# The low parts of the expert weights: GpSimd's quarter goes to VectorE

## The chip, the cores and the metric

The kernel runs on one core of one Trainium2 chip. The metric is the device time of one execution in microseconds (us), the median of several runs. The engines are TensorE (PE in the profile, its weight loads PEld), VectorE (DVE), ScalarE (ACT), GpSimd (POOL) and SyncE (SP), which issues DMAs.

## The reference

One layer of a decoder over 1024 tokens of width 1024, all in fp32. Three sublayers follow each other: token mixing (sparse attention beside a recurrent mixer), cross-attention into 256 memory tokens, and a mixture of experts. Only the last one matters here:

```
s = sigmoid(x @ router_w)                      # 16 experts, in 4 groups
group = best group of each token; e = its top-2 experts
gate = s[e] / sum(s[e])
y = sum over the two e of gate * ((silu(x @ w_gate[e]) * (x @ w_up[e])) @ w_down[e])
x = layer_norm(alpha * x + y)
```

Each of the 16 experts has three weights of 1024 x 512 values, 2 MB each.

## The kernel before

**Split products.** A product of fp32 matrices is made of three matrix multiplications on rounded values. A value v is split into a high part, hi = v rounded to the type fp32r, and a low part, lo = v - hi. `mm3` (L35 to L37) sums hi*hi, hi*lo and lo*hi into one PSUM bank; for some rows two products are enough (L1591, L1639, L1640).

**The experts.** `Experts.load` (L1519) fetches half of a weight, 1 MB, from HBM into a buffer `wraw` of 128 x 2048 values, by a DMA on SyncE's queue. `parts` forms its hi (`whi`) and lo (`wlo`) in CUT = 4 pieces of 128 x 512: ScalarE casts a piece to `whi` (L1528), then VectorE or GpSimd subtracts (L1529):

```
for i in range(CUT):
    cs = slice(n * i, n * i + n)
    nc.scalar.copy(hi[:, cs], raw[:, cs])
    (nc.gpsimd if i in LOPOOL else nc.vector).tensor_tensor(lo[:, cs], raw[:, cs], hi[:, cs].bitcast(F32), ALU.subtract)
```

There are 16 experts x 6 halves x 4 pieces = 384 such pieces; 8 of them are formed early, near 1364 us, while the cross-attention's output is still under way (`early`). The others go LOOK = 4 halves ahead of their use. Two halves of a weight, eight pieces, are taken as a pair.

**One expert** (`expert`). Its tokens are gathered by an indirect DMA of GpSimd (`exg`, L1551) once GpSimd has worked out their indices in five small steps (`ef` and `eix`, L1542 to L1546). TensorE turns them (`etp`, L1558), ScalarE and VectorE split them into `exh` and `exl` by `split` (L28; for the second set of rows into the two halves of `exr`), TensorE multiplies with gate and up weights (`eacc`), ScalarE and VectorE form silu times up (`eth`, L1578, L1579, L1601), which is turned and split into `ehh` and `ehl` (`ehr` for the second set), and multiplied with the down weight. ScalarE scales the result (`ey`, L1627) and GpSimd adds it to the sum in HBM by an indirect DMA (`accd`, L1632). Eight experts have a second, smaller set of rows. After the last experts the layer norm runs over the rows of `accd` (statistics `lnst` L978, then L987 and L992), and the last two experts' rows are normed on their own and scattered to the output (L1635).

**Order.** The code is traced in the order in which it is written, and a planner (`schedule_with_timeline_sim=True`) then lays out the instructions of each engine by its own costs and due times. Each engine runs its instructions in the order laid out.

Of the kernel before, what the change touches and what calls it, by code (L numbers as in the profile page):

```python
# [1252 lines left out]
GROUPS = (4, 7, 8)  # L1253
FIRST = (14, 6, 6, 6, 6, 6, 6, 7)
HOLD = 4
CUT, LOPOOL = 4, (2,)
LATE = 2


# [653 lines left out]
```

## Time and profile before

| | us |
|---|---|
| median of 3 runs | 1892.65 |
| lowest, highest | 1884.31, 1894.74 |
| profiled execution | 1896.58 |
| its span, first to last instruction | 1894.7 |
| busy: PE, DVE, ACT, POOL | 1759.3, 1321.1, 858.6, 698.1 |
| mean granted TensorE clock, of full speed | 0.959 |

The profiled execution is one further run. Its span is what the profile's views divide up; its own time is 1.9 us longer. The experts' products run from about 1430 us to 1866 us, and the layer norm at the end overlaps the last ones.

### The profile page before, as it was taken

Reading aid. Unit: us, or ns where it says so; the run is one execution under the profiler, and the core shown is the slowest. Engines: PE = TensorE matmul, PEld = TensorE weight load, DVE = VectorE, ACT = ScalarE, POOL = GpSimd, SP = SyncE. Lnnn points to the kernel's source line nnn. Section 1 sums busy time; section 2 is a strip of 40 time slices with the busy share of each in tenths; the row PEclk is TensorE's granted clock in tenths of the full one; section 3 lists DMA queues with packets and bytes.
Section 4 is the critical chain, followed back from the end, with each engine's and each line's share of the span. In section 5 each row is a group of like instructions: output and inputs, shape, how many; then the busy total and the mean of one; then the engine's idle time right before and its main releaser. Section 6 shows DMA issues by size and latency. Waiting matters only on the chain. (4 is left out here: it accounts for less than half of the span.)

```text
span 1894.7 us, 27396 instructions
## 1 busy us (share of the span) xinstructions
PE 1759.3 (93%) x9158; PEld 1433.4 (76%) x9158; DVE 1321.1 (70%) x2767; ACT 858.6 (45%) x1775; POOL 698.1 (37%) x780
## 2 busy tenths in 40 slices
PE   8999999999999899999999789999998999999991
PEld 6877777777687787888887577878787888877871
DVE  3225876888777621498987575546987788989876
ACT  4223313434332222298887441024414666667662
POOL 1123202221221121175747122100346576656556
PEclk9999989999999899999999899999989999999995
DMA  7363434444432226812101765133325999899984
GB/s 232 110 186 105 118 142 124 135 128 121 108 111 87 67 89 198 255 43 75 46 8 36 226 211 172 34 97 123 117 107 172 332 325 309 278 294 302 332 269 152
DMA packets 246143, 301.98 MB, mean 159 GB/s; under 512 B 54653, under 2 KB 142741, under 8 KB 245488
## 3 DMA queue, kind: packets, MB, share of 16 engines
q1 hardware_dynamic: 238016, 273.59, 44.4%
q0 software_dynamic: 7984, 26.62, 5.7%
q8 instruction: 73, 1.20, 0.3%
q14 instruction: 70, 0.57, 0.1%
HBM read 234.05 MB, written 70.98 MB: 161 GB/s over the span
## 5 line engine op out<-in xcount | busy, mean ns | idle before, releaser
L1529 DVE TENSOR_TENSOR wlo<-wraw,whi 128x512 fp32r<-128x512 f32 x288 | 281.1, 1026 | 26.1 <-ACT whi L1528 25.7
L35 PE MATMUL acc<-xh,wh 128*128 128x512 f32 (+1 forms) x656 | 273.6, 417 | 5.9 <-ACT wh L117 3.0
L36 PE MATMUL acc<-xl,wh 128*128 128x512 f32 (+1 forms) x656 | 267.1, 408 | 0.0
L37 PE MATMUL acc<-xh,wl 128*128 128x512 f32 (+1 forms) x656 | 266.6, 408 | 0.2 <-POOL wl L118 0.2
L1528 ACT CAST whi<-wraw 128x512 fp32r<-128x512 f32 x384 | 207.8, 623 | 35.4 <-PE eacc L1591 10.2
L118 POOL TENSOR_TENSOR wl<-wraw,wh 128x1024 fp32r<-128x1024 f32 (+1 forms) x41 | 100.8, 2459 | 308.6 <-ACT wh L117 259.2
L35 PEld LDWEIGHTS acc<-xh,wh 128*128 128x128 f32 (+1 forms) x656 | 125.1, 191 | 45.3 <-issue 8.0
L1529 POOL TENSOR_TENSOR wlo<-wraw,whi 128x512 fp32r<-128x512 f32 x96 | 138.8, 1482 | 46.4 <-ACT whi L1528 40.5
L37 PEld LDWEIGHTS acc<-xh,wl 128*128 128x128 f32 (+1 forms) x656 | 124.6, 190 | 33.7 <-issue 5.2
L36 PEld LDWEIGHTS acc<-xl,wh 128*128 128x128 f32 (+1 forms) x656 | 125.0, 191 | 29.8 <-issue 3.1
L851 DVE TENSOR_TENSOR tinv<-xinv,ln 128x248 f32<-128x248 f32 (+30 forms) x248 | 89.3, 360 | 40.6 <-DMA ln<-ld 15.6
L475 ACT ACTIVATE pp<-pp,nm 128x640 f32<-128x640 f32 (+7 forms) x128 | 94.3, 740 | 9.3 <-DVE nm L474 8.1
L28 DVE TENSOR_TENSOR pl<-ptp,ph 128x512 fp32r<-128x512 f32 x132 | 87.4, 685 | 12.0 <-ACT ph L28 11.3
L36 PE MATMUL eacc<-wlo,exh 128*128 128x512 f32 x240 | 94.2, 392 | 0.2 <-DVE wlo L1529 0.2
L35 PE MATMUL eacc<-whi,exh 128*128 128x512 f32 x240 | 94.2, 393 | 0.0
L37 PE MATMUL eacc<-whi,exl 128*128 128x512 f32 x240 | 94.2, 392 | 0.0
L480 POOL TENSOR_SCALAR pp<-pp,wgt 128x640 f32<-128x640 f32 (+7 forms) x128 | 88.4, 711 | 0.6
L852 DVE TENSOR_TENSOR xinv<-xinv,tinv 128x248 f32<-128x248 f32 (+30 forms) x248 | 84.0, 339 | 5.9
L980 POOL TENSOR_SCALAR lnrs<-lnmv 128x1 f32<-128x1 f32 x21 | 19.7, 936 | 180.5 <-DVE lnmv L979 172.6
L28 ACT CAST ph<-ptp 128x512 fp32r<-128x512 f32 x132 | 73.8, 583 | 16.9 <-PE ptp L534 16.1
L534 PE MATMUL ptp<-ident,pp 128*128 128x128 f32 x528 | 79.2, 276 | 0.4 <-DVE pl L28 0.2
L909 ACT COPY state<-rseq 64x64 f32<-64x64 f32 x128 | 26.8, 209 | 116.4 <-PE rseq L905 97.5
(502 smaller groups left out, 4542.9 us busy)
## 6 DMA issues: line engine op xcount, KB each, us to landing
wraw<-in_moe_w_up SPq DMA_DIRECT2D x32, 1024.0 KB
wraw<-in_moe_w_gate SPq DMA_DIRECT2D x32, 1024.0 KB
wraw<-in_moe_w_down SPq DMA_DIRECT2D x32, 1024.0 KB
wraw<-in_w_in SPq DMA_DIRECT2D x40, 512.0 KB
sm<-ev SPq DMA_DIRECT2D x32, 256.0 KB
sr<-ev SPq DMA_DIRECT2D x28, 256.0 KB
skew<-skew SPq DMA_DIRECT2D x1, 4608.0 KB
xraw<-in_x SPq DMA_DIRECT2D x8, 512.0 KB
```

The source lines that it names most:

```text
L28: x = nc.scalar.copy(hi, src), (nc.gpsimd if by_pool else nc.vector).tensor_tensor(lo, src, hi.bitcast(F32), ALU.subtract)
L35: nc.tensor.matmul(out, ah, bh, start=start, stop=False)
L36: nc.tensor.matmul(out, ah, bl, start=False, stop=False)
L37: nc.tensor.matmul(out, al, bh, start=False, stop=stop)
L118: nc.gpsimd.tensor_tensor(wl, raw, wh.bitcast(F32), ALU.subtract)
L475: nc.scalar.activation(pt[:, :n], pt[:, :n], AF.Exp, bias=nm, scale=-1.0, accum_out=sums[:, 0, i:i + 1])
L480: nc.gpsimd.tensor_scalar(st[br, i][:, :n], st[br, i][:, :n], w[:, 0, i:i + 1], 1.0, ALU.mult, ALU.mult)
L534: nc.tensor.transpose(tp[:, 128 * i:128 * i + 128], st[br, i][:, c0:c0 + 128], ident)
L851: nc.vector.tensor_tensor(tmp[:, :, :w], x[:, :, j:j + 1].to_broadcast([128, 8, w]), ln[:, j:j + 1, j + 1:].to_broadcast([128, 8, w]), ALU ...
L852: nc.vector.tensor_tensor(x[:, :, j + 1:], x[:, :, j + 1:], tmp[:, :, :w], ALU.subtract)
L1528: nc.scalar.copy(hi[:, cs], raw[:, cs])
L1529: (nc.gpsimd if i in LOPOOL else nc.vector).tensor_tensor(lo[:, cs], raw[:, cs], hi[:, cs].bitcast(F32), ALU.subtract)
```

## The change

The constant that tells which of the four pieces go to GpSimd is emptied. Piece 2 of each half, 96 in all, is now subtracted by VectorE like the other three. Nothing else in the code changes; the planner lays out all instructions anew.

```diff
 HOLD = 4
-CUT, LOPOOL = 4, (2,)
+CUT, LOPOOL = 4, ()
 LATE = 2
```

## Rows read from the trace of the kernel before

**Rows 1.** The page's head: the span, and busy time, share of the span and instructions of each engine.
```profile
span 1894.7 us, 27396 instructions
PE 1759.3 (93%) x9158; PEld 1433.4 (76%) x9158; DVE 1321.1 (70%) x2767; ACT 858.6 (45%) x1775; POOL 698.1 (37%) x780
```

**Rows 2.** Busy time by stretch: the stretch, its length, busy us (and instructions) of PE, PEld, DVE, ACT, POOL, then the granted clock, the DMA engines' busy share and GB/s.
```profile
1445.00:1838.00 393.00, 382.95 (x1824) 313.90 (x1824) 333.09 (x396) 268.74 (x516) 246.33 (x248) 0.99 0.94 303
...
1640.00:1690.00 50.00, 47.49 (x225) 39.31 (x224) 44.51 (x49) 31.14 (x61) 29.77 (x32) 0.97 0.96 298
...
1840.00:1895.00 55.00, 14.00 (x48) 9.99 (x48) 39.04 (x43) 18.27 (x29) 33.37 (x29) 0.65 0.55 186
```

**Rows 3.** What TensorE waits for from 1445 to 1838 us (total us, times, longest), and the row of its timeline at 1441 us (start, us; in brackets the idle time before it and what ended it).
```profile
PE etp L1558 <- DMA exg<-x2d,eix: 3.2, 2, 2.5
PE eacc L1639 <- DVE ehr L28: 2.7, 6, 0.9
PE eacc L1591 <- DVE exr L28: 2.1, 2, 1.7
PE etp L1558 <- PE etp L1558: 1.0, 2, 0.8
PE eacc L35 <- ACT ehh L28: 0.7, 1, 0.7
PE eacc L36 <- DVE wlo L1529: 0.2, 1, 0.2
...
1441.21 1.97 PE L1558 MATMUL etp<-ident,exg 128*128 128x128 f32 x8 [5.01 <-DMA exg<-x2d,eix]
```

**Rows 4.** The low parts: the page's groups by engine (count | busy us, mean ns | idle before), and from the tile's own view the least, median and greatest duration in ns.
```profile
L1529 DVE TENSOR_TENSOR wlo<-wraw,whi 128x512 fp32r<-128x512 f32 x288 | 281.1, 1026 | 26.1 <-ACT whi L1528 25.7
L1529 POOL TENSOR_TENSOR wlo<-wraw,whi 128x512 fp32r<-128x512 f32 x96 | 138.8, 1482 | 46.4 <-ACT whi L1528 40.5
...
L1529 DVE TENSOR_TENSOR wlo<-wraw,whi x288: 639/682/4751, 1363.6 to 1845.1; 128x512 fp32r<-128x512 f32 x144
L1529 POOL TENSOR_TENSOR wlo<-wraw,whi x96: 1261/1357/1861, 1364.7 to 1837.9; 128x512 fp32r<-128x512 f32 x96
```

**Rows 5.** Timeline, merged runs (start, us, count): a run of two low parts on VectorE with none on GpSimd beside it, a run of six, and GpSimd's low parts beside that run.
```profile
1560.14 1.29 DVE L1529 TENSOR_TENSOR wlo<-wraw,whi 128x512 fp32r<-128x512 f32 x2 [2.77 <-ACT whi L1528]
...
1652.31 7.93 DVE L1529 TENSOR_TENSOR wlo<-wraw,whi 128x512 fp32r<-128x512 f32 x6
...
1655.31 3.77 POOL L1529 TENSOR_TENSOR wlo<-wraw,whi 128x512 fp32r<-128x512 f32 x3
```

**Rows 6.** Timeline of VectorE, GpSimd and TensorE near 1364 us, where the first pieces are formed.
```profile
1364.84 3.98 DVE L1529 TENSOR_TENSOR wlo<-wraw,whi 128x512 fp32r<-128x512 f32 x3
1368.74 0.68 DVE L1236 SCALAR_TENSOR_TENSOR x<-x,xwo 128x512 f32<-128x512 f32 x1
...
1366.79 1.48 POOL L1529 TENSOR_TENSOR wlo<-wraw,whi 128x512 fp32r<-128x512 f32 x1 [0.80 <-ACT whi L1528]
...
1369.46 0.50 PE L35 MATMUL xwo<-xoh 128*128 128x512 f32 x1 [1.69 <-DVE x L1236]
```

**Rows 7.** The same near 1461 us.
```profile
1461.60 5.86 DVE L1529 TENSOR_TENSOR wlo<-wraw,whi 128x512 fp32r<-128x512 f32 x6
...
1465.44 1.48 POOL L1529 TENSOR_TENSOR wlo<-wraw,whi 128x512 fp32r<-128x512 f32 x1 [2.01 <-ACT whi L1528]
...
1467.85 0.51 PE L1591 MATMUL eacc<-whi,exr 128*128 128x512 f32 x1 [1.68 <-DVE exr L28]
```

**Rows 8.** Timeline of ScalarE, GpSimd and TensorE, 1638 to 1661 us: the result y, GpSimd's queue up to the next gather, and the turn that needs it.
```profile
1638.00 0.69 ACT L1627 ACTIVATE ey<-eacc,ef 128x512 f32<-128x512 f32 x1
...
1639.91 1.29 POOL L1529 TENSOR_TENSOR wlo<-wraw,whi 128x512 fp32r<-128x512 f32 x1
...
1641.29 1.28 POOL L1529 TENSOR_TENSOR wlo<-wraw,whi 128x512 fp32r<-128x512 f32 x1
1642.74 1.87 POOL L1632 DMA_INDIRECT accd<-ey,eix  x1 [0.17 <-issue]
...
1653.49 0.18 POOL L1543 CAST eix<-ef 128x1 int32<-128x1 f32 x1 [3.67 <-DMA accd<-ey,eix]
...
1654.24 1.05 POOL L1551 DMA_INDIRECT exg<-x2d,eix  x1 [0.44 <-POOL eix L1546]
...
1660.77 2.20 PE L1558 MATMUL etp<-ident,exg 128*128 128x128 f32 x12 [2.51 <-DMA exg<-x2d,eix]
```

**Rows 9.** Timeline of VectorE and GpSimd where the last low parts are formed.
```profile
1839.04 1.29 DVE L978 BATCH_NORM_STATS2 lnst<-wraw 128x6 f32<-128x512 f32 x2 [6.24 <-DMA wraw<-accd]
...
1840.83 1.28 DVE L1529 TENSOR_TENSOR wlo<-wraw,whi 128x512 fp32r<-128x512 f32 x2
...
1836.60 2.54 POOL L1529 TENSOR_TENSOR wlo<-wraw,whi 128x512 fp32r<-128x512 f32 x2
```

**Rows 10.** What SyncE's queue waits for from 1440 to 1845 us (total us, times, longest).
```profile
SPq L1519 <- DVE wlo L1529: 165.6, 71, 8.5
```

**Rows 11.** GpSimd's small steps: one kind of index step from 1445 to 1838 us (count | busy us, mean ns), one of them alone at 1435 us, and the gathers' least, median and greatest duration in ns.
```profile
L1544 POOL TENSOR_SCALAR ef<-ef,dum 128x1 f32<-128x1 f32 x20 | 13.3, 664 | 1.3
...
1435.01 0.34 POOL L1544 TENSOR_SCALAR ef<-ef,dum 128x1 f32<-128x1 f32 x1
...
L1551 POOL DMA_INDIRECT exg<-x2d,eix x23: 1017/1053/1493, 1436.8 to 1806.4; - x23
```

## Prediction

> **What bounds the kernel now.** I read the page's busy shares first [rows 1], then the table of stretches [rows 2] to find the stage that the change touches, then what TensorE waits for in that stage [rows 3], and last the changed instructions themselves [rows 4 to 11]. The page alone says that TensorE is busy for 93% of the span and VectorE for 70%. The stretch 1445 to 1838 us, which is the experts' stage after its start, says more: TensorE is busy 382.95 of 393 us, VectorE 333.09, ScalarE 268.74, GpSimd 246.33, and the DMA engines 94% [rows 2]. So TensorE sets this stage and VectorE has 60 us of room in it. What the change can give there is bounded by TensorE's idle time: 3.2 + 2.7 + 2.1 + 1.0 + 0.7 + 0.2 = 9.9 us, plus what a lowered clock costs behind an idle stretch. Of these waits only 0.2 us are for a low part itself; the others are for small conversions by VectorE (ehr, exr) and for gathered rows (exg) [rows 3].
>
> The reader should see next that the low part has two speeds on VectorE: its median is 682 ns, its mean 1026 and its maximum 4751 [rows 4]. The long ones lie beside GpSimd's low parts: a run of two without GpSimd takes 1.29 us, a run of six takes 7.93 us while GpSimd makes three of its own in 3.77 us [rows 5]. Over 288 the excess is 288 x (1.026 - 0.682) = 99 us of VectorE's time.
>
> The Trainium skill names the mechanism in "SBUF — State Buffer", section "Who interferes with whom": a VectorE instruction with two SBUF inputs contends with a GpSimd instruction that reads SBUF, and the later one blocks until the first is done. This trace agrees, with 682 ns without and up to 4751 ns beside such a neighbour.
>
> **The change part by part.** It takes 96 low parts off GpSimd, which are 138.8 us of its busy time (mean 1482 ns) [rows 4], and adds 96 to VectorE. No byte, matmul, cast or DMA changes in number.
>
> *Price of one on VectorE.* In a run two take 1.29 us [rows 5] and a single one 0.68 [rows 4], so one more costs 0.61. The upper bound is what one occupies on average today, 281.1 / 288 = 0.976 us [rows 4]. I take 0.61, since GpSimd's neighbour, which makes it 0.976, is gone. VectorE then spends 384 x 0.61 = 234 us on low parts instead of 281: it is relieved by 47 us although it makes a third more of them. A set of eight (two halves of a weight) takes 8 x 0.61 = 4.9 us where six take 6 x 0.976 = 5.9 on average. VectorE stays off the bound: 333 - 47 = 286 of 393 us.
>
> The Trainium skill, "VectorE: DVE Perf Modes", section "The TRN2 errata", has a formula for an fp32 two-input instruction that gives 691 ns for 512 elements, and its section on the drain lets no next one start before. By that the 384 would take 265 us, an estimate. The rows show that the next one starts after 0.61 us in a run; by either price VectorE is relieved.
>
> *What this gives, place by place.*
> 1. Start of the parts, at 1364 us: three low parts take 3.98 us beside GpSimd's, the x behind them starts at 1368.74, and TensorE waits 1.69 us for it [rows 6]. With GpSimd's part among them there are four at 0.61, which ends at 1367.3: -1.5 us.
> 2. At 1461 us: six take 5.86 us, and TensorE waits 1.68 us for the exr behind them [rows 7]. Eight take 4.9: -1.0 us.
> 3. The other waits for ehr and exr come to 2.7 + 2.1 - 1.7 = 3.1 us [rows 3]. The runs ahead of them lie beside GpSimd's low parts as well; I take two thirds: -2.0 us.
> 4. The gather at 1654.24 us. Its chain runs back over GpSimd's in-order queue: the rows y were ready at 1638.69, but the scatter started only at 1642.74, with two low parts ahead of it (1639.91 and 1641.29, together 2.57 us). The next index waits until 1653.49 for that scatter's DMA, then comes the gather, and TensorE stands 2.51 us [rows 8]. Without the two low parts the scatter leaves some 2.5 us sooner, and so does all behind it: -2.5 us. The granted clock of that stretch is 0.97 [rows 2]; the missing 3% of 50 us are 1.5 us, which come back with the wait: -1.5 us.
> 5. The other gather that TensorE waits for has 3.2 - 2.5 = 0.7 us [rows 3]: -0.7 us.
> 6. The end. Two of GpSimd's low parts at 1836.60 lie beside VectorE's waiting time; VectorE does its last ones behind the statistics of 1839.04, which wait 6.24 us for a load [rows 9]. From there to the end VectorE is the busiest (39.04 of 55 us) [rows 2], so two more in its queue cost up to 2 x 0.61: +1.2 us. The cover for them would be the idle 6.24 us ahead, if they stand before the statistics; I don't count on it.
>
> Sum: -1.5 - 1.0 - 2.0 - 4.0 - 0.7 + 1.2 = -8.0 us. The 5.01 us wait at 1441 us stays: its gather goes out before GpSimd has made any low part of this stage [rows 3].
>
> *Work costed at nothing.* The loads of raw weights start when a buffer comes free, and SyncE waits 165.6 us for VectorE's low parts [rows 10]; sooner frees make earlier loads. That gives nothing, since no wait of TensorE is for a weight beyond the 0.2 us. If this cover went, the DMA engines at 94% would be next. What is queued behind the added low parts on VectorE is eth, exl, exr, ehl and ehr; TensorE waits for those.
>
> **Rivals.**
> *More comes back.* TensorE loses nearly all its idle time of the stage (9.9 us), the 1.5 us of clock, the 1.5 us of place 1, and the end gains about 3 us as well because the scatters ahead of it leave sooner: about -16 us, 1877. For it: each place has GpSimd in its chain. Against it: waits for transposes and for ScalarE (1.0 + 0.7 us) do not.
>
> *Nothing that can be seen.* The stage is 97% TensorE and the gathers are paced by the scatters' landings, so that an earlier scatter meets another wait: 0 to -3 us, about 1891. For it: only 9.9 us are there to take, in many small places.
>
> *Slower by VectorE's queue.* The order of instructions is written by a planner that reckons with the costs of each engine, so the added low parts can be placed ahead of a conversion that TensorE needs soon, and where no GpSimd part slowed VectorE, eight take 1.2 us longer than six. The place is the experts' loop, 48 sets of eight. If a third of the sets cost TensorE 1.2 us, that is 16 x 1.2 = +19 us against the -8: +11, about 1904. It decides from seven sets on (7 x 1.2 = 8.4). If the low part even kept its 0.976 us, the 94 in the stretch would bring VectorE to 333 + 92 = 425 of 393 us and it would become the bound: +32 us, 1925. That decides from where an added low part costs VectorE over (393 - 333) / 94 = 0.64 us with the others at today's price. Against both: the long ones have GpSimd's beside them, which goes.
>
> *Slower by GpSimd's small steps.* A denser stream on VectorE holds up the index arithmetic and the descriptors on GpSimd. For it: an index step of one column takes 0.34 us alone and 664 ns on average in this stage, and the gather takes from 1017 to 1493 ns [rows 11]. If each of five steps and the gather lost another 0.68 us, a gather would be 4 us late; at the six or so that come just in time this is 6 x 4 = +24 us less the 8: +16, 1909. It decides where the added delay exceeds the 2.5 us that the two low parts free. Against it: VectorE's time in low parts falls, from 281 to 234 us.
>
> The Trainium skill has this rule, in "SBUF — State Buffer", section "SBUF: two separate sides": VectorE's instructions that hold the shared ports keep GpSimd from writing descriptors, so that a DMA issued there looks blocked. It ties that to a mode which this instruction does not have, so I give it a small chance.
>
> **How the numbers follow.** The profiled execution took 1896.58 us, 1.9 more than its span and 3.9 more than the median of the three runs. Its sum is 1896.6 - 8.0 = 1888.6; the same step from the median 1892.65 gives 1884.6, and I say 1885. Chances: this forecast 0.42 (its own range 1878 to 1891), more comes back 0.30, nothing 0.10, VectorE's queue 0.10, GpSimd's steps 0.08. Half a percent, 9.5 us, is about what a measurement can tell here (the three runs spread over 10.4 us). Faster by more than that: 0.30 and a fifth of the forecast, 0.38. Slower: 0.18. Within: 0.44. The range runs from 1868 (9.9 us of idle time, 1.5 of clock, 1.5 of place 1, 5 at the end, and 7 for the scatter of the runs, whose lowest is 8.3 below their median) to 1904 (the mild case of VectorE's queue); what lies outside is part of the slow cases and a little below, under 0.2.
>
> **What would show it.** Right: low parts on VectorE with mean near their median of 682 ns and no maximum above 1 us; VectorE's busy time in 1445 to 1838 down by some 40 us; no wait for exg near 1660 us and the clock there at 1.00. Wrong: a mean still near 1 us; waits for ehl, ehr or exr that grow; gathers that take longer; or a TensorE busy time and end of stage that stand where they were.

## The result, and the profile after

The changed kernel takes 1917.47 us (median of 4 runs, 1914.59 to 1920.21) beside 1893.0 of the kernel before on the same chip: ratio 1.0138, 95% interval 1.0103 to 1.0174. It is slower by 24.5 us where I forecast 8 us less. The profiled execution took 1915.71 us.

The page's head of the changed kernel and its groups of low parts, and from the tile's own view their least, median and greatest duration:

```profile
span 1913.9 us, 27190 instructions
PE 1752.1 (92%) x9158; PEld 1429.2 (75%) x9158; DVE 1279.3 (67%) x2863; ACT 858.4 (45%) x1775; POOL 568.8 (30%) x684
...
L1529 DVE TENSOR_TENSOR wlo<-wraw,whi 128x512 fp32r<-128x512 f32 x384 | 238.0, 683 | 33.3 <-ACT whi L1528 33.3
...
L1529 DVE TENSOR_TENSOR wlo<-wraw,whi x384: 642/683/700, 1350.7 to 1859.8; 128x512 fp32r<-128x512 f32 x192
```

Beside [rows 1, 4] the change does what it says. VectorE makes a third more low parts in 238.0 us instead of 281.1, none is longer than 700 ns, and GpSimd has lost 129 us. No engine got more to do, and the kernel is longer. So the time must be waiting. The same stretches as in [rows 2], and what TensorE waits for as in [rows 3]:

```profile
1445.00:1838.00 393.00, 368.48 (x1738) 304.19 (x1737) 273.89 (x461) 251.03 (x482) 105.58 (x142) 0.97 0.88 287
1640.00:1690.00 50.00, 49.34 (x239) 40.68 (x239) 38.29 (x65) 35.52 (x69) 17.20 (x25) 1.00 0.97 317
```

```profile
PE etp L1558 <- DMA exg<-x2d,eix: 22.3, 6, 6.1
PE eacc L1639 <- DVE ehr L28: 1.8, 4, 1.1
PE eacc L1591 <- DVE exr L28: 0.4, 1, 0.4
```

TensorE was busy for 382.95 of these 393 us and is now busy for 368.48. The waits for VectorE's conversions fell (ehr and exr from 4.8 to 2.2 us), those for gathered rows grew from 3.2 to 22.3, and the granted clock went from 0.99 to 0.97. Where the time is lost is told by three timelines.

**A. The order on TensorE.** The end of one expert and the turns of the next, first in the kernel before, then in the changed one:

```profile
1704.54 1.90 PE L1610 MATMUL etq<-ii,egr 128*128 128x64 f32 x16
1706.24 0.48 PE L35 MATMUL eacc<-whi,ehh 128*128 128x512 f32 x1
...
1712.78 1.06 PE L1558 MATMUL etp<-ident,exg 128*128 128x128 f32 x8 [0.70 <-DMA exg<-x2d,eix]
```

```profile
1704.68 1.90 PE L1610 MATMUL etq<-ii,egr 128*128 128x64 f32 x16
1711.73 1.09 PE L1558 MATMUL etp<-ident,exg 128*128 128x128 f32 x4 [5.16 <-DMA exg<-x2d,eix]
1712.47 0.78 PE L35 MATMUL eacc<-whi,ehh 128*128 128x512 f32 x1
...
1720.25 1.47 PE L1558 MATMUL etp<-ident,exg 128*128 128x128 f32 x12
```

Before, the 24 down products (ehh, ehl) came first, and the gathered rows landed while they ran. Now the planner has put four turns of the next expert's rows ahead of those ready products. TensorE works through its queue in order, so it stands 5.16 us for a gather that lands no later than before (1711.60 against 1712.64). The products behind it then run at the lower of the clock's two levels at first: 0.78 us for the first one, where it was 0.48. The changed kernel has this order at four places, and at three of them (1604, 1711, 1820 us) TensorE waits 5.2 to 6.1 us.

**B. The start.** GpSimd, VectorE and TensorE of the changed kernel where the first expert's tokens are gathered, then busy times by stretch (columns as in [rows 2]) where that gather lands, of after and of before:

```profile
1421.73 5.13 POOL L1544 TENSOR_SCALAR ef<-ef,dum 128x1 f32<-128x1 f32 x1
1426.81 0.18 POOL L1546 CAST eix<-ef 128x1 int32<-128x1 f32 x1
1427.14 1.04 POOL L1551 DMA_INDIRECT exg<-x2d,eix  x1 [0.15 <-POOL eix L1546]
...
1421.92 4.89 DVE L1529 TENSOR_TENSOR wlo<-wraw,whi 128x512 fp32r<-128x512 f32 x8
...
1434.75 1.97 PE L1558 MATMUL etp<-ident,exg 128*128 128x128 f32 x8 [14.31 <-DMA exg<-x2d,eix]
```

```profile
1430.00:1445.00 15.00, 9.21 (x38) 7.65 (x39) 6.35 (x12) 5.97 (x12) 5.67 (x15) 0.65 1.02 381
```

```profile
1436.00:1445.00 9.00, 3.92 (x13) 3.03 (x13) 4.32 (x15) 2.75 (x6) 5.11 (x15) 0.70 0.33 75
```

An index step of one column, 0.34 us when alone [rows 11], lasts 5.13 us: it ends (1426.86) with VectorE's unbroken run of eight low parts beside it (1426.81). The gather leaves 4.8 us late, at 1427.14. By then the loads of the next weights go out as well (1427.40 and 1430.13), the DMA engines are full (1.02 from 1430 on, against 0.33), and the gather needs 7.6 us to land where before it needed 4.4 (issued at 1436.80, landed by 1441.21). That the loads slow it is my reading; the gather of [rows 8], in the full stage of the kernel before, needed 6.4 us too. The wait of 5.01 us [rows 3] has become 14.31.

**C. The end.** VectorE and GpSimd of the changed kernel, then of the kernel before; TensorE's last instruction ends at 1880.2 and 1866.0 us:

```profile
1886.64 3.36 DVE L992 SCALAR_TENSOR_TENSOR wraw<-wraw,lnrs,eexr 128x1024 f32<-128x1024 f32 x1 [2.22 <-POOL lnrs L981]
1889.93 0.74 DVE L1629 SCALAR_TENSOR_TENSOR exg<-eacc,ef,exg 128x512 f32<-128x512 f32 x1
...
1896.94 1.75 POOL L1635 DMA_INDIRECT out<-exg,eix  x1 [0.53 <-issue]
```

```profile
1870.55 3.36 DVE L987 SCALAR_TENSOR_TENSOR exg<-exg,lnmv,exgr 128x1024 f32<-128x1024 f32 x1
1873.84 1.40 DVE L1629 SCALAR_TENSOR_TENSOR exg<-eacc,ef,exg 128x512 f32<-128x512 f32 x2
...
1877.30 1.04 POOL L1635 DMA_INDIRECT out<-exg,eix  x1 [0.83 <-DVE exg L992]
```

The first of the two last scatters goes out 16.7 us after TensorE's end instead of 11.3: the last result is added (L1629) later, behind another row block's norm (L992), and more of the norm stands behind it. The tail from TensorE's last instruction to the end of the trace is 33.7 us instead of 28.7.

The profile's sum: between the first product of a gathered second set (exr) and TensorE's last instruction lie 441.7 us instead of 422.7 (+19.0), the tail has +5.0. The first such product comes 4.8 us earlier (1438.5 against 1443.3), in spite of B, since the work ahead of the experts ran some 13 us earlier in this execution: its first output product of the cross-attention (`xwo`) starts at 1301.6 us instead of 1314.3, when no low part has been formed yet. A kernel with the old split shows such an early start too (1434.5 in e6), so I give that to neither side. 19.0 + 5.0 - 4.8 = 19.2, the difference of the spans.

### The profile page after: what moved, and what is told of

Same layout as the page of the kernel before. It is cut to its first block, busy times and chain, and to the rows that moved or that the text cites. A ratio compares the mean times of both kernels' runs of the same rounds, so it can differ in the third digit from the quotient of the medians.

```text
span 1913.9 us, 27190 instructions
## 1 busy us (share of the span) xinstructions
PE 1752.1 (92%) x9158; PEld 1429.2 (75%) x9158; DVE 1279.3 (67%) x2863; ACT 858.4 (45%) x1775; POOL 568.8 (30%) x684
## 5 line engine op out<-in xcount | busy, mean ns | idle before, releaser
L1529 DVE TENSOR_TENSOR wlo<-wraw,whi 128x512 fp32r<-128x512 f32 x384 | 238.0, 683 | 33.3 <-ACT whi L1528 33.3
L37 PEld LDWEIGHTS acc<-xh,wl 128*128 128x128 f32 (+1 forms) x656 | 124.6, 190 | 33.9 <-issue 5.1
L1632 POOL DMA_INDIRECT accd<-ey,eix x32 | 51.8, 1618 | 164.0 <-ACT ey L1627 105.9
L28 DVE TENSOR_TENSOR pl<-ptp,ph 128x512 fp32r<-128x512 f32 x132 | 87.3, 684 | 11.9 <-ACT ph L28 11.3
```

Source lines behind the costliest of these rows:

```text
L28: x = nc.scalar.copy(hi, src), (nc.gpsimd if by_pool else nc.vector).tensor_tensor(lo, src, hi.bitcast(F32), ALU.subtract)
L37: nc.tensor.matmul(out, al, bh, start=False, stop=stop)
```

## The experiments

Theory: the changed order on TensorE (A) and the held-up index step (B) make the loss, and under them the change gives what it was costed to give. Rivals: VectorE's added low parts hold up TensorE; the loss is GpSimd's small steps all along the stage; the gain was never there.

**e1_order, again as e9_order_again.** The changed kernel with an edge for the planner: the turns of an expert's main rows stand behind the last main down product of the expert ahead. Nothing is computed otherwise.

```diff
+BEHIND = ('m',)
 for q in range(0 if first else 2):
-    k.split(self.turned(ps, main[2], q)...)
+    with ExitStack() as st:
+        if self.behind is not None:
+            st.enter_context(k.tc.issue_after(self.behind))
+        tp = self.turned(ps, main[2], q)
+    k.split(tp...)
...
-                    mm(o, f, *wt[d])
+                    last = mm(o, f, *wt[d])
+                if tag in BEHIND:
+                    self.behind = last
```

> The changed kernel, with one edge on TensorE's order: the turns of an expert's gathered main rows stand behind the last main product with the down weight that was traced before them. In the changed kernel four of these turns stand ahead of 24 such products at three later places, and TensorE idles 5.5, 5.2 and 6.1 us there. Theory 'order of TensorE' (the emptied GpSimd queue let the planner expect the gather sooner and put its turns ahead of ready work): the three waits shrink to the 0.7 to 2.5 us that stand at the same place in the kernel before, and the low clock behind them goes: 12 to 18 us under the changed kernel, 1899 to 1905 us. Rival 'start' (the loss is the 14.3 us wait near 1421 us): under 3 us. Rival 'VectorE' (its longer sets of eight low parts hold up what TensorE needs): under 3 us, about 1917.

> The same kernel as e1_order (the change, turns of an expert's main rows behind the last main down product of the expert ahead), timed again beside e10 and e11. About 1903 us, ratio near 1.003, the wait of some 13 us at the start still in it.

Measured: 1903.36 us, ratio 1.0031 (1.0003 to 1.0059), and again 1898.36, 1.0035 (1.0016 to 1.0053). Of 1.38 points 1.03 to 1.07 are gone, some 20 us, and the stage fell from 441.7 to 416.3 and 419.7 us. VectorE makes the same 384 low parts. So the order on TensorE was the larger part of the loss, and the rival "VectorE's added work" falls. The start's waits stay: 2.7 and 10.0 us in e1, 4.5 and 8.7 in e9. The second of each pair is for four turns of the next expert's rows, which stand ahead of the first expert's exr products, in the changed kernel too (1437.76 us, where the wait is 1.04). The edge does not reach these turns.

**e2_index.** The changed kernel with the first expert's ten index steps on VectorE (`eng` is `nc.vector` in `rows` for the first list, `nc.gpsimd` for all others).

```diff
-        self.lists = [self.list(r, REG * r) for r in range(FIXED)]
+        self.lists = [self.list(r, REG * r, self.k.nc.vector) for r in range(FIXED)]
```

> The changed kernel, with the ten index steps of the first expert's two lists on VectorE and not on GpSimd. In the changed kernel one such step takes 5.13 us on GpSimd, beside a run of eight low parts on VectorE that takes 4.89 us, and the gather behind it collides with the next weight loads. Theory 'start' (GpSimd's small step is locked out by the run): the wait of 14.3 us falls back to some 5 us, 8 to 12 us under the changed kernel, 1905 to 1909. Theory 'order of TensorE' alone: no difference. Rival 'VectorE': ten more steps on VectorE, no gain or a loss of 1 to 2 us.

Measured: 1926.51 us, ratio 1.0127 (1.0086 to 1.0168). The start's wait fell to 4.20 us, as theory B says, but the time did not fall. TensorE's waits from 1400 to 1860 us:

```profile
PE etp L1559 <- DMA exg<-x2d,eix: 32.4, 8, 5.6
```

The edit moved the plan again. Three of the later waits (1555.6, 1670.3 and 1782.5 us, 4.6 to 5.6 us each) are for turns ahead of down products, as in A; one (1524.1) is for turns ahead of exr products; two (1618.5 and 1731.2, 4.3 and 3.2 us) are for turns that stand behind the down products, as before. Alone this run says nothing of what the start costs.

**e3_order_r.** The edge of e1, and the turns also behind the second set's sixteen products (ehr).

```diff
-BEHIND = ('m',)
+BEHIND = ('m', 'r',)
```

> As e1_order, but the turns stand behind the products of the second set of rows too, 16 more. Theory 'order of TensorE': the gather gets 3.9 us more before TensorE needs it, so the waits for gathered rows after the start go to nothing, at the price of a gap of up to 2 us between the turns and the next products: 15 to 25 us under the changed kernel, 1893 to 1902. If it is slower than e1_order, the gap costs more than the waits. Rival 'VectorE': about 1917.

Measured: 1896.27 us, ratio 0.9993 (0.9973 to 1.0013). Waits for gathered rows are left at the start alone (3.3 and 10.5 us). The stage is no shorter than in e1 (419.0 us); what is gained lies in the tail, 23.7 us.

**e4_both, again as e5_both_again.** The changed kernel with the edits of e2 and e3.

> e2_index and e3_order_r together. If both theories hold and add up: 25 to 35 us under the changed kernel, 1883 to 1892, at or under the kernel before (1893), since VectorE is also relieved. If one of them explains the same time as the other: no better than the better of the two. Rival 'VectorE': about 1917.

> The same kernel as e4_both (the change, with the order of TensorE held and the first expert's index steps on VectorE), timed again beside e6_before_both. Theory (the change relieves VectorE and GpSimd by what I worked out, and the loss comes only from the new order and from the held-up index step): about 1888 us, 0.4 to 0.6% below before, and some 8 us below e6_before_both. Rival (the change gives nothing once the order is held): level with e6_before_both.

Measured: 1888.12 us, ratio 0.9945 (0.9916 to 0.9973), and again 1880.39, 0.9914 (0.9885 to 0.9944). This version beats both kernels. Its stretch from 1545 to 1795 us, and below it the same of the kernel before:

```profile
1545.00:1795.00 250.00, 250.00 (x1207) 206.67 (x1207) 191.41 (x323) 176.32 (x337) 81.27 (x104) 1.00 0.99 320
```

```profile
1545.00:1795.00 250.00, 243.63 (x1163) 199.83 (x1162) 218.69 (x253) 168.48 (x324) 151.23 (x158) 0.99 0.96 306
```

TensorE has no idle moment and the full clock in these 250 us, and issues 1207 products instead of 1163.

**e6_before_both.** The kernel before with the edits of e4.

> The kernel before (a quarter of the low parts on GpSimd) with the same two edits as e4_both: turns of gathered rows behind the down products of the expert ahead, the first expert's index steps on VectorE. Theory: the order of before was already this one, so the edges change nothing there; 1890 to 1900 us, ratio 0.995 to 1.003, low parts on VectorE of mean near 1.0 us, and some 8 us above e5_both_again. Rival (all of the gain of e4_both is from the two edits): level with e5_both_again, 0.5% below before.

Measured: 1909.26 us, ratio 1.0078 (1.0053 to 1.0102); 29 us above e5. My expectation rested on a wrong reading: before has twelve turns between the main products and those of the second set, and this edge takes them out of that gap. TensorE's two largest waits from 1445 to 1838 us:

```profile
PE eacc L1647 <- DVE ehr L28: 10.9, 6, 4.3
PE eacc L1597 <- DVE exr L28: 4.0, 3, 1.8
```

As I read it, VectorE's conversions are late with GpSimd's low parts beside them (its low parts last up to 5549 ns here), and the turns that covered it are gone. So this order is good only with the change; the pair does not give the worth of the change under the order of before, which e10 and e11 were made for.

**e7_gp_too** and **e8_neither**: what tips the planner? In e7 GpSimd makes its 96 low parts too, into the same place, and VectorE writes them again. In e8 no engine makes them, and the products take the high part in their place.

```diff
+            if i == 2:
+                nc.gpsimd.tensor_tensor(lo[:, cs], raw[:, cs], hi[:, cs].bitcast(F32), ALU.subtract)
```

> The change, but GpSimd makes its 96 low parts as well, into the same place, and VectorE writes them again behind it: the plan has GpSimd as loaded as before and VectorE as loaded as after. Theory that GpSimd's emptied queue alone makes the planner move the turns ahead: few turns stand ahead, waits for gathered rows in the experts' stage (1445 to 1838 us) below 8 us in all. Theory that VectorE's longer sets in the plan do it: waits as in the changed kernel, 20 us or more. In both the low parts on VectorE become long again beside GpSimd's (mean near 1 us, so 384 of them take about 380 us), and the time lies above the kernel after's for that reason if VectorE becomes the bound: 1900 to 1935 us.

> Leaves out the low parts of piece 2 altogether: no engine makes them, and the hi part stands in their place in the products, whose number stays. So GpSimd is as empty as after, VectorE has its 288 low parts as before and no GpSimd low part beside them. Theory that the loss comes from GpSimd's emptied queue by way of the planner's order: turns stand ahead of ready products at some places, waits of 4 to 6 us each for gathered rows, time 1895 to 1915 us, although VectorE has 58 us less to do than after (96 x 0.61). Theory that the loss comes from VectorE's added work: no such waits, 1875 to 1888 us.

Measured: e7 1966.02 us, ratio 1.0365 (1.0308 to 1.0422), above the 1900 to 1935 that I expected, with 53.0 us of waits for gathered rows from 1380 us on, in 7 places. GpSimd's queue is as full in the plan as before, and the turns stand ahead all the same; but from 1445 us on VectorE waits 46.8 us for GpSimd's low parts, which neither kernel does, so the run is no clean copy of its plan. e8: 1901.35 us, ratio 1.0017 (0.9989 to 1.0044). What TensorE waits for from 1445 to 1838 us in e8:

```profile
PE etp L1567 <- DMA exg<-x2d,eix: 21.0, 6, 6.2
```

That is the figure of the changed kernel (22.3 in 6), although VectorE has a quarter less of this work. The stage, from the first exr product to TensorE's last instruction, is as long too: 441.6 us beside 441.7. So the emptied GpSimd is enough to tip the order, and the added low parts do not lengthen the stage. e7 shows the order tipped with GpSimd as full as before, but there each of VectorE's added low parts has to follow one of GpSimd's, so that VectorE's load alone would do it is not shown. Which of the planner's comparisons tips stays open.

**e10_before_order** and **e11_order_index**: the kernel before with the edge of e1; and the changed kernel with the edge of e1 and the index steps of e2.

> The kernel before with the edge of e1_order alone: TensorE's order at the ends of the experts was the same already, so the change and its undoing are compared here under one order. Theory (edge harmless; the change gives back what I worked out, 8 us, and costs some 9 us at the start): ratio 0.997 to 1.002, within 3 us of e9 on either side, and 5 to 10 us above e11. Rival (the edge itself is worth the 1% that e1 gained): as much below the kernel before, ratio near 0.99.

> The change with the edge of e1_order and the first expert's index steps on VectorE, without the further edge of e3. Theory: 8 to 12 us below e9 (the start's wait falls from 13 to about 5 us), ratio 0.993 to 0.998. Rival (the start's wait is hidden behind something later): level with e9.

Measured: e10 1891.33 us, ratio 0.9991 (0.9970 to 1.0013); e11 1890.0 us, 0.9985 (0.9965 to 1.0005); e9 beside them 1.0035. The edge is worth nothing to the kernel before, so what e1 gained was the undoing of the changed order. e10 lies 7 us below e9 and not within the 3 us that I expected; e11 lies 8.4 us below e9, where I expected 8 to 12 (and e4 8.2 below e3, by the same edit), which is what the start costs, held step and turns ahead together: in e11 and e4 the exr products come first again. I expected e10 5 to 10 us above e11; it is 1.3. Under one order and with the start mended, the change is worth 0.06 points, about 1 us, less than the intervals can tell. The traces, one execution each, say what may hide in it:

| kernel | low parts on GpSimd | first exr product at | stage, us | tail, us |
|---|---|---|---|---|
| before | 96 | 1443.3 | 422.7 | 28.7 |
| e10 | 96 | 1440.1 | 421.4 | 28.0 |
| after | 0 | 1438.5 | 441.7 | 33.7 |
| e1, e9 | 0 | 1443.8, 1443.7 | 416.3, 419.7 | 33.4, 32.8 |
| e11 | 0 | 1436.8 | 418.2 | 33.5 |
| e3 | 0 | 1447.4 | 419.0 | 23.7 |
| e4, e5 | 0 | 1436.7, 1436.3 | 418.4, 418.7 | 23.6, 23.6 |

The stage runs from the first product of a second set (exr) to TensorE's last instruction. With the order of before the changed split shortens it by some 4 us (mean of e1, e9 and e11 418.1, of before and e10 422.1; the three spread over 3.4 us), and the end takes 5 us back. That longer tail goes with the added low parts: it is 32.8 to 33.9 us in the changed kernel, e1, e2, e9 and e11, and 27.2 in e8, which lacks them. e4 and e5 gain their 10 us over e11 in the tail alone: there TensorE stands 16.6 us in two waits near the end (8.7 for eth, 7.9 for ehl), and meanwhile VectorE gets the other rows' norm done: its last L992 of those ends 0.8 us after TensorE's last instruction in e5 and 9.8 us after it in the changed kernel. Why the planner lays the end out in this way was not tried.

**e12_start_only.** One part of the change: VectorE makes all low parts of the first six halves, GpSimd its quarter of the other 90.

```diff
-            (nc.gpsimd if i in LOPOOL else nc.vector).tensor_tensor(...)
+            (nc.gpsimd if i in (2,) and len(self.done) >= 6 else nc.vector).tensor_tensor(...)
```

> One part of the change alone: piece 2 of the first six halves is VectorE's (the first expert's weights, formed from 1350 to 1430 us), of the other 90 halves GpSimd's, as before. Theory (the start's loss comes from runs of eight on VectorE that hold up GpSimd's index steps): a wait for gathered rows of 10 us or more near 1430 us, low parts of the stage again of mean near 1 us, time 5 to 12 us above before, ratio 1.003 to 1.007. Rival (the start costs nothing, the loss is all in the stage's order): level with before.

Measured: 1902.08 us, ratio 1.0043 (1.0020 to 1.0065), some 8 us, the size that I expected, with six low parts moved. The start's wait is two waits, 4.90 and 8.67 us. Its index step beside a run of eight and the gather behind it, VectorE's last split of exr, and TensorE:

```profile
1432.26 4.78 POOL L1545 TENSOR_TENSOR ef<-ef 128x1 f32<-128x1 f32 x1
...
1438.22 1.02 POOL L1551 DMA_INDIRECT exg<-x2d,eix  x1 [0.22 <-POOL ef L1544]
...
1437.84 0.42 DVE L28 TENSOR_TENSOR exr<-etp,exr 128x256 fp32r<-128x256 f32 x1 [0.43 <-ACT exr L28]
...
1435.43 1.97 PE L1558 MATMUL etp<-ident,exg 128*128 128x128 f32 x8 [4.90 <-DMA exg<-x2d,eix]
1446.07 1.08 PE L1558 MATMUL etp<-ident,exg 128*128 128x128 f32 x4 [8.67 <-DMA exg<-x2d,eix]
1446.81 0.77 PE L1591 MATMUL eacc<-whi,exr 128*128 128x512 f32 x1
```

Another kind of step is held, by as much. It stands in GpSimd's queue ahead of the index steps of the next expert's rows, so their gather leaves late, at 1438.22. But the exr rows are split by 1438.26, and their products stand idle until 1446.81 only because four turns of the next expert's rows are ahead of them in TensorE's queue. So most of the start's wait here, as in e1, e3 and e9, is the held step and the order of A together. What the held step would cost with the exr products first was not tried.

## Why the prediction was wrong, point by point

- **Price of a low part, 0.61 us.** Right. Eight take 4.89 us, 0.611 each; VectorE's 238.0 us stand beside the 234 reckoned, and not the estimate of 265. For that one I left out what the Trainium skill's "VectorE: DVE Perf Modes", section "The DRAIN you can't avoid", says as well: a next instruction that is not held starts earlier. The trace agrees, with 0.60 us from one start to the next beside a duration of 0.68. The rule of the Trainium skill that names the neighbour on GpSimd ("SBUF — State Buffer", "Who interferes with whom") holds as far as VectorE goes: without that neighbour no low part of the changed kernel lasts over 700 ns.
- **Place 1.** Right: TensorE no longer waits for the x behind the first run (1.7 us gone, 1.5 reckoned).
- **Places 2 and 3.** Right in size: ehr and exr fell by 2.6 us, 3.0 reckoned.
- **Places 4 and 5.** Wrong in sum. At the old place the wait did fall (2.51 us, now 0.66 at 1662.51) and the clock came back (0.97, now 1.00 from 1640 to 1690), but I took the other gathers as fixed. GpSimd, without low parts, now waits for the landing of the scatter ahead, and another gather comes late, at a place where the turns stand behind the products as before (GpSimd, then TensorE, of the changed kernel):

```profile
1543.64 0.53 POOL L1543 CAST eix<-ef 128x1 int32<-128x1 f32 x1 [7.43 <-DMA accd<-ey,eix]
1544.11 0.66 POOL L1546 CAST eix<-ef 128x1 int32<-128x1 f32 x1
1544.93 1.33 POOL L1551 DMA_INDIRECT exg<-x2d,eix  x1 [0.16 <-POOL eix L1546]
...
1553.17 2.73 PE L1558 MATMUL etp<-ident,exg 128*128 128x128 f32 x12 [4.39 <-DMA exg<-x2d,eix]
```

  With order and start mended (e11) 6.8 us of such waits are left behind the start, where before had 3.2. That is the reason that I gave the rival "nothing that can be seen".
- **"The wait at 1441 us stays".** Wrong, by 9.3 us in the profile and some 8 us by e12 and by e9 against e11 (there together with the turns ahead of the exr products). I looked at GpSimd's own queue, which had no low part there, and not at what VectorE does beside it. I had the mechanism as a rival ("GpSimd's small steps") at 0.08, with the right condition, more than 2.5 us of delay; but I had put 0.68 us on every step, and what came was one step held for 5.13. I set the rival aside because VectorE's total time in low parts falls. A total says nothing of one step that meets a run.
- **Earlier loads costed at nothing.** Wrong at the start as I read it, where they go out together with the late gather (1.02 of the DMA engines, 7.6 instead of 4.4 us to land).
- **The order of TensorE.** The step that failed most, 20 us, and it stands in no line of the sum: I took each engine's order as given. The rival with the planner, at 0.10, saw only the order on VectorE. But in the experts' loop nothing that was added to VectorE hurt (e8's stage is as long without it); the planner moved TensorE's order, which the change does not touch.
- **Place 6, the end.** Sign right, size wrong: 5.0 us, not 1.2. I counted two low parts in VectorE's queue; what came was another order of the norm.

Of the forecast gain of 8 us the traces show about 6 (4 in the stage, 1.7 at place 1), which no comparison of times sets apart; against them stand 20 us of order, 9 of the start and 5 of the end. Their sum, 28, is near the 24.5 measured.

## What to carry to other kernels

Where a planner lays out the instructions, a change of an engine's load is a change of every engine's order: before trusting a sum of local gains, look for the places where ready work stands next to work that waits for a transfer, and hold that order with an edge. A fair test of a change is then change and original under one held order, as e9 to e11 were. Work that is light but on the path, such as an index step in front of a gather, is worth a look where it meets a long run on another engine: moving ten such steps to VectorE gave 8 us, twice, once TensorE's order was held.

## What the runs showed of the hardware

In five kernels one small GpSimd step lasted until the end of VectorE's run of eight low parts beside it (4.89 us) at the first expert's start: 5.13 us in the changed kernel, 4.95 in e9, 4.78 in e12, and, begun later in the run, 3.37 in e1 and 2.81 in e3, against 0.34 or 0.2 alone. I had expected a delay of one instruction, 0.68. The rule in "SBUF — State Buffer", "Who interferes with whom" of the Trainium skill speaks of the one instruction that holds the ports; in these five the step did not come in between two of them.

The run's length does not decide it. Some 18 us later in the changed kernel two steps come in between the parts of another run of eight:

```profile
1440.11 4.89 DVE L1529 TENSOR_TENSOR wlo<-wraw,whi 128x512 fp32r<-128x512 f32 x8
...
1440.94 0.50 POOL L1545 TENSOR_TENSOR ef<-ef 128x1 f32<-128x1 f32 x1
1441.50 0.54 POOL L1546 CAST eix<-ef 128x1 int32<-128x1 f32 x1
```

In e5 ten steps do so in a run of nineteen (1437.19 to 1448.72 us), at 0.33 to 1.83 us each. All these runs are as dense: a low part starts every 0.60 us and lasts 0.68. What made the first run hold a step to its end stays open.

Each wait of 5 us costs more than its length: behind the 5.16 us at 1711 the stretch 1690 to 1740 has a granted clock of 0.93, behind the 6.1 us at 1820 the stretch 1790 to 1840 has 0.90, where the kernel before had 1.00 in both. In the 250 us of e5 in which TensorE never waited it was 1.00 throughout.
